# Weight tiles in a pool of their own at the bottom of SBUF, in a one-layer diffusion backbone with split fp32 matmuls

## The chip, the cores and the metric

The kernel runs on one core of one Trainium2 chip. The metric is the device time of one execution in microseconds (us), of which the median over several executions counts. A profile of one execution comes with it: every instruction with its start and duration, the clock that TensorE was granted, and the DMA traffic.

## The reference

One layer over 512 latent tokens of width 1024, with 256 context tokens beside them; everything is fp32.

```python
hx = modulate(rms_norm(x, norm1_g[i]), sh1, sc1)
qx, kx, vx, ux, gx = project(hx, w_in[i], q_norm_g[i], k_norm_g[i])
...
attn_x = block_attention(qx, concat([kc, kx]), concat([vc, vx]))
mix_x = merge_branches(attn_x, ux, gx, w_attn_out[i], conv_dw_w[i], ..., w_conv_out[i], w_out[i])
x = x + g1 * mix_x
hx2 = modulate(rms_norm(x, norm2_g[i]), sh2, sc2)
x = x + g2 * conv_glu_ffn(hx2, w_up[i], ffn_dw_w[i], ffn_dw_b[i], w_down[i])
return rms_norm(x, final_g)
```

`merge_branches` gates the attention branch and a convolution branch (GLU, width-31 depthwise convolution, layer norm, swish), and projects their sum. The feed forward goes up to two halves of 2816 channels, convolves one with width 3, and comes down again. The modulation (`sh1`, `sc1`, `g1`, `sh2`, `sc2`, `g2`) is a matrix-vector product.

## The kernel before

**Split operands.** TensorE multiplies in a 4-byte format with fewer significant bits than fp32. So each operand is split into two parts, `hi` and `lo`: ScalarE casts the source (L180), VectorE subtracts (L181). A product is then three matmuls, `mm3` (L203 to L205): hi by hi, hi by lo, lo by hi. A matmul has a stationary operand (`lhsT`, 128 columns, put into the array by a LDWEIGHTS of its own before each matmul) and a moving operand (`rhs`, mostly 512 columns). In the profile's names, `acc<-s,hl` is a matmul whose moving operand lies in a tile `s` and whose stationary operand lies in a tile `hl`.

**Where operands lie.** Activations live in 19 slots `s0` to `s18`, each [128, 2, 512] of 4 bytes, that is 4,096 bytes of each partition: 2,048 for hi, 2,048 for lo. Weights come as 1 MB chunks by DMA into `raw` (three buffers of 8,192 bytes, issued by SyncE) and are split into `hl` tiles, [128, 2, 1024], 8,192 bytes each, in four buffers taken in turn (`weights`, L191). Few more operands lie elsewhere: `ex`, `e0`, `e1` (three more slots for the gates and the feed forward), `y`, `plo`, `pT` (attention probabilities and parts of the values), `va`, `vb` (values).

**The order in the partition.** The allocator lays pools one behind the other in the order in which they are opened, and the tiles of a pool in the order in which they are first asked for. Pool `cst` is opened first and `wp` second. The build of the kernel before gives these byte offsets in each partition:

| what | pool | from | to | start modulo 64 |
|---|---|---|---|---|
| s0 to s18 | cst | 16,512 | 94,336 | 0 |
| cb0 to cb3 | cst | 94,336 | 111,232 | 0 |
| vecs, ident, ones, ..., va, vb, part | cst | 111,232 | 125,792 | va: 32 |
| raw, 3 buffers | wp | 125,792 | 150,368 | 32 |
| hl, 4 buffers | wp | 150,368 | 183,136 | 32 |
| y, 2 buffers | yp | 183,136 | 191,328 | 32 |
| ex, e0, e1 (among others) | rows, fp | 195,424 | 207,712 | 32 |

**The order of the work.** It is written out by hand. First the modulation, the normed rows `hx` (slots s0 to s7) and the first convolution channels; then k, v and q; then attention head by head, with the other half of q, the last convolution channels and the gates of branch a as fillers between the heads' steps, while VectorE runs the 124 taps of the convolution in what it has left; then the gates and branches; the output projection (`out_proj`, L903: stationary operand in `M`, the slots s0 to s7, moving operand in the slots s11 to s18, s8 to s10, in `ex` and in `hl`); then the feed forward in groups of 11, 7 and 4 channel tiles. In it, `up` (L968) has weights `hl` as the stationary and the slots s0 to s7 as the moving operand; `down` (L980) has channel slots `act` as the stationary operand (s8 to s18, then ex, e0, e1, then s8 again) and `hl` as the moving one. Dependencies between engines become semaphore waits that the framework writes; a buffer is handed on when its last reader is done.

Of the kernel before, what the change touches and what calls it, by code (L numbers as in the profile page):

```python
# [9 lines left out]
F32 = mybir.dt.float32  # L10
F32R = mybir.dt.float32r
# [4 lines left out]
P = 128  # L16
D = 1024
KT = D // P
T = 512
# [5 lines left out]
CT = CONV // P  # L25
TAPS = 31
# [6 lines left out]
GROUPS = ((0, 11), (11, 7), (18, 4))  # of the feed forward's channel tiles  # L33
CB = 2 * 512 + 32

# The order of the work: what keeps the tensor engine fed.
# start: m: modulation of two row tiles, x: tokens, r: rows, w: weights, a b: products
FIRST = "m0 x0 r0 m1 w0 a0 r1 m2 w1 r2 a1 b0 m3 r3 a2 b1 a3 b2 b3"
WHOLE = (("sh1", 0), ("sc1", 0), ("sc1", 1))  # modulation over the whole tensor engine
# q: query rows, u: a quarter of a channel tile | s: scores, f: filler  # L40
Q_ORDER = "quqqq|uusfufsfsfsf"
KV_LAG, Q_LAG = 3, 3  # of the transposes
# taps of the convolution: per step before attention, in a head's steps, in the gates'
# [3 lines left out]
EARLY, AHEAD = 48, 6  # the tap at which the second modulation starts, its loads before  # L47
HEAD_FILL = (2, 4, 5, 4, 5, 4, 4, 4)  # first step of a head with a filler
PV_FIRST = (3, 4, 5)  # heads with the values before the next scores
# gates' steps: the layer norm's stages, the second modulation's sums and results  # L50
# [4 lines left out]
# vecs columns  # L55
# [15 lines left out]
def layout(inp):  # L71
# [3 lines left out]
    # even members of a rotary pair first, within each head  # L75
# [69 lines left out]
    # rotary tables: constants of the shapes  # L145
# [14 lines left out]
def body(tc, x_d, ctx_d, wts_d, vecs_d, rows_d, rope_d, out_d, at):  # L160
# [9 lines left out]

    cst = pool("cst")
    wp = pool("wp")
    # [P, 2, T]: both parts of an operand of the tensor engine
    slot = [cst.tile([P, 2, T], F32R, name=f"s{i}") for i in range(19)]
    # convolution input and sum per channel tile; x before that, the residual after
    cbuf = [cst.tile([P, CB], F32, name=f"cb{i}") for i in range(CT)]

# [11 lines left out]
    done = []  # the latest weights' split  # L189

    def weights(name, w, n=CH):  # L191
        raw = fetch(name, n)
        out = []
        for o in range(0, n, 1024):
            m = min(1024, n - o)
            t = wp.tile([P, 2, 1024], F32R, tag="hl", name="hl", bufs=4)
            done[:] = split(raw[:, o : o + m], t[:, 0, :m], t[:, 1, :m])
            out.append(t[:, :, :m].rearrange("p a (k c) -> p a k c", c=w))
        return out
# [26 lines left out]
    def rsqrt(dst, ss, n, f=1.0):  # L226
        """dst = ((ss / n + eps) * f) ** -0.5"""
        V.tensor_scalar(dst, ss, f / n, f * EPS, ALU.mult, ALU.add)
        G.tensor_tensor(dst, dst, mhalf[:, : dst.shape[1]], ALU.pow)

    # silu of both conditioning vectors, side by side per row tile
# [5 lines left out]
    bs = cst.tile([P, 16], F32, name="bs")  # 1 + bias of the two scales  # L237
    V.tensor_scalar(bs[:, 0:8], vcol(V_BMOD + 8, 8), 1.0, None, ALU.add)
    V.tensor_scalar(bs[:, 8:16], vcol(V_BMOD + 32, 8), 1.0, None, ALU.add)
    cwh = vcol(V_CW, CT * TAPS)  # halved: the gate below is doubled  # L240
# [6 lines left out]
    def gemv_steps(part, r, k0, c):  # L247
        """part += sum over row tiles k0.. of r[:, k] * conditioning c"""
        for k in range(r.shape[1]):
            s = cs[:, k0 + k, c : c + 1]  # L250
            if k0 + k == 0:
                yield V.tensor_scalar(part, r[:, k], s, None, ALU.mult)
            else:
                yield V.scalar_tensor_tensor(part, r[:, k], s, part, ALU.mult, ALU.add)  # L254
# [12 lines left out]
    def half_row(name, jj):  # L267
        """Partial sums of 512 outputs of the modulation."""
        part = new_part()
        for h in range(2):  # L270
            raw = fetch((name, 2 * jj + h))
            gemv(part, raw.rearrange("p (k c) -> p k c", c=512), 4 * h, 0)
        return part
# [4 lines left out]
    def mod2(i):  # L278
        """Sixths of the modulation of the second half, with the first gate."""
        parts[i] = half_row(*sixths[i])  # L280
# [10 lines left out]
    def gate_row(pt, dst, part, j, f):  # L291
        """Half j of a gate, over all partitions; its bias is in dst."""
        PE.matmul(pt, lhsT=ones, rhs=part, start=True, stop=True)
        d = dst[:, 512 * j : 512 * j + 512]
        V.tensor_tensor(d, pt, d, ALU.add)
        if f != 1.0:
            V.tensor_scalar(d, d, f, None, ALU.mult)
# [7 lines left out]
    # ================= latent and context rows, q, k, v =================  # L305
# [6 lines left out]
    # values: both parts for the first group's heads  # L312
# [14 lines left out]
    mark = [None]  # the vector engine's latest step  # L327
# [4 lines left out]
    def head_scale(src, n, f, rs, junk):  # L332
        """rs: what scales each of n heads of src to unit rms (over sqrt(f))"""
        ss = small(4, "ssq")
        for h in range(n):
            S.activation(junk[:, tok(h)], src[:, tok(h)], AF.Square, accum_out=ss[:, h : h + 1])
        rsqrt(rs, ss[:, :n], HD, f)
# [9 lines left out]
    # queries stay as they are: their scale enters with the exponential  # L347
# [21 lines left out]
    with ExitStack() as p0:  # L369
# [4 lines left out]
        def kv_norm(src, s):  # L374
            """keys of token tile s (0-3 latent, 4-5 context), values alongside"""
            rs, qn = small(4, "rsq"), kt()
            head_scale(src, 2, 1.0, rs[:, :2], qn)
            for h in range(2):
                S.activation(qn[:, tok(h)], src[:, tok(h)], AF.Copy, scale=rs[:, h : h + 1])
            split(src[:, 256:384], vs[s][0], vlo[:, s])  # L380
            S.copy(vs[s][1], src[:, 384:512])
            if s < TT:
                return roped(qn, 2, s, TABk, kt(), qn)
            qn = heads(qn)
            mark[0] = V.tensor_tensor(qn, qn, gq[:, 1:2, :].broadcast_to([P, 2, HD]), ALU.mult).ins
            return qn
# [21 lines left out]
        # both conditioning vectors for a column tile of the tensor engine; the sum of the four  # L408
# [8 lines left out]
        def mod_rows(name, j):  # L417
            """256 outputs of the modulation, a row per conditioning vector; in each of the
            column tiles from two of the row tiles, or, while data is awaited, from all at once"""
            r = fetch((name, j)).rearrange("p (k c) -> p k c", c=256)  # L420
            pt = acc()
            if (name, j) in WHOLE:
                n = 2
                for k in range(KT):
                    PE.matmul(pt[0:n, 0:256], lhsT=cs[:, k], rhs=r[:, k], start=k == 0, stop=k == KT - 1)  # L425
            else:
                n = P
                for k in range(KT):
                    q = 32 * (k % 4)
                    PE.matmul(  # L430
                        pt[q : q + 32, 0:256], lhsT=cs4[:, k], rhs=r[:, k], start=k < 4, stop=k >= 4,
                        tile_position=(0, q),
                    )
            row = sp.tile([n, 256], F32, tag="row", name="row", bufs=2)
            V.tensor_copy(row, pt[0:n, 0:256])
            return row, sel if n == P else ident[0:2, 0:2]
# [6 lines left out]
        # the first channel tiles of the convolution branch follow the rows as they come  # L443
# [3 lines left out]
        def mod_x(j):  # L447
            """Modulation of channel tiles 2j and 2j+1."""
# [58 lines left out]
        # context rows  # L507
# [3 lines left out]
        # rotary tables with the gains  # L511
# [11 lines left out]
        def conv_taps():  # L523
            """depthwise over tokens, a tap at a time"""
# [8 lines left out]
        def conv_steps():  # L533
            """The taps, with the first sixth of the second modulation among them."""
# [15 lines left out]
        def conv(n):  # L550
            """The next n taps, queued behind the vector engine's latest step."""
            with tc.issue_after(mark[0]):
                for _ in range(n):
                    next(taps, None)
# [3 lines left out]
        # the first half of the weights in the places of q  # L558
# [15 lines left out]
        def tick():  # L574
            """The transposes that are due."""
# [60 lines left out]
    # ================= attention =================  # L636
    with ExitStack() as p1:
# [63 lines left out]
        def values(h, s, pT):  # L701
# [4 lines left out]
            if s == 5:  # L706
                split(pv[h], qT[h][:, 0], qT[h][:, 1])  # in the place of q
# [31 lines left out]
    # ================= gates, branches =================  # L739
# [38 lines left out]
    # layer norm over the convolution's channels, swish  # L778
# [20 lines left out]
    def ln_var(s_):  # L799
        """the variance as a column per token"""  # L800
# [7 lines left out]
    def ln_out(s_):  # L808
        """its power spread over the partitions again"""
# [74 lines left out]
    # ================= output projection (token major), residual =================  # L884
# [57 lines left out]
    # ================= feed forward =================  # L942
# [40 lines left out]
    def last_rows(t, w, f0, nf):  # L983
        """The last group's part, the final norm and the output."""
# [22 lines left out]
    # the first channel tiles start on the tokens that are ready  # L1007
# [52 lines left out]
```

## Time and profile before

| what | value |
|---|---|
| median of 3 runs | 852.66 us (852.2 to 852.67) |
| span of the profiled execution, first to last instruction | 851.1 us |
| median less this span | 1.6 us |
| matmuls, PE busy | 3948, 832.9 us (98% of the span) |
| VectorE busy | 566.6 us (67%) |
| ScalarE busy | 362.2 us (43%) |
| granted TensorE clock, mean over the span | 0.995 |

The profiled execution's own time is this span and what lies outside the first and the last instruction, 1.6 us if it was the median one. Matmuls are pipelined: one shows 395 ns from its start to its end, but the next starts about 230 ns after it. What a matmul costs TensorE is therefore the step from one start to the next. A row of the timeline gives starts to 0.01 us, so a step is read over many matmuls in a row.

### The profile page before, as it was taken

Reading aid. Unit: us, or ns where it says so; the run is one execution under the profiler, and the core shown is the slowest. Engines: PE = TensorE matmul, PEld = TensorE weight load, DVE = VectorE, ACT = ScalarE, POOL = GpSimd, SP = SyncE. Lnnn points to the kernel's source line nnn. Section 1 sums busy time; section 2 is a strip of 40 time slices with the busy share of each in tenths; the row PEclk is TensorE's granted clock in tenths of the full one; section 3 lists DMA queues with packets and bytes.
Section 4 is the critical chain, followed back from the end, with each engine's and each line's share of the span. In section 5 each row is a group of like instructions: output and inputs, shape, how many; then the busy total and the mean of one; then the engine's idle time right before and its main releaser. Section 6 shows DMA issues by size and latency. Waiting matters only on the chain.

```text
span 851.1 us, 10190 instructions
## 1 busy us (share of the span) xinstructions
PE 832.9 (98%) x3948; PEld 668.9 (79%) x3948; DVE 566.6 (67%) x979; ACT 362.2 (43%) x700; POOL 25.2 (3%) x50
## 2 busy tenths in 40 slices
PE   6999999999999999999999999999999999999996
PEld 3578888778888777888888988877888888888875
DVE  3478878999999996964854467745244555346555
ACT  4454455789776232423515643332122233213333
POOL 1001010000000000000000000000000000000001
PEclk9999999999999999999999999999999999999998
DMA  9861112020103345673730133432222222222102
GB/s 355 298 258 53 50 54 95 4 97 1 50 1 134 119 162 204 232 262 102 271 122 0 51 130 142 178 145 87 86 99 99 99 100 87 86 99 99 50 1 100
DMA packets 16177, 99.25 MB, mean 117 GB/s; under 512 B 1792, under 2 KB 2048, under 8 KB 6144
## 3 DMA queue, kind: packets, MB, share of 16 engines
q1 hardware_dynamic: 15120, 95.98, 30.7%
q10 hardware_dynamic: 1008, 2.62, 0.9%
q8 instruction: 31, 0.51, 0.2%
q14 instruction: 18, 0.15, 0.1%
HBM read 96.49 MB, written 2.10 MB: 116 GB/s over the span
## 4 chain that ended last, share of the span: by engine, by line
PE 92%; DVE 3%; ACT 2%; DMA 1%; issue 1%; POOL 0%; POOLq 0%; SPq 0%
PE acc L203 25%; PE acc L205 24%; PE acc L204 24%; PE bank L204 3%; PE bank L205 3%; PE bank L203 3%; PE tr L714 2%; DMA raw<-in_wts 1%; PE sc L203 1%; PE sc L205 1%; PE sc L204 1%; PE acc L425 1%; PE tr L402 1%; PE acc L430 1%; PE acc L265 0%
## 5 line engine op out<-in xcount | busy, mean ns | idle before, releaser
L203 PE MATMUL acc<-s,hl 128*128 128x512 f32 (+1 forms) x632 | 244.4, 388 | 0.6 <-ACT s L180 0.6
L204 PE MATMUL acc<-s,hl 128*128 128x512 f32 (+1 forms) x632 | 242.1, 383 | 0.0
L205 PE MATMUL acc<-s,hl 128*128 128x512 f32 (+1 forms) x632 | 242.0, 383 | 0.0
L181 DVE TENSOR_TENSOR hl<-raw,hl 128x1024 fp32r<-128x1024 f32 x118 | 139.0, 1184 | 79.1 <-ACT hl L180 78.9
L180 ACT CAST hl<-raw 128x1024 fp32r<-128x1024 f32 x118 | 119.7, 1022 | 153.6 <-PE acc L205 134.6
L203 PEld LDWEIGHTS acc<-s,hl 128*128 128x128 f32 x632 | 118.2, 188 | 27.1 <-ACT s L180 0.9
L204 PEld LDWEIGHTS acc<-s,hl 128*128 128x128 f32 x632 | 118.6, 188 | 26.2 <-issue 1.2
L205 PEld LDWEIGHTS acc<-s,hl 128*128 128x128 f32 x632 | 118.5, 188 | 25.9
L531 DVE SCALAR_TENSOR_TENSOR cb<-cb,vecs 128x512 f32<-128x512 f32 x120 | 88.3, 744 | 1.1
L203 PE MATMUL acc<-hl,s 128*128 128x512 f32 (+1 forms) x212 | 83.3, 393 | 0.2 <-DVE tmp L342 0.2
L204 PE MATMUL acc<-hl,s 128*128 128x512 f32 (+1 forms) x212 | 82.9, 391 | 0.0
L205 PE MATMUL acc<-hl,s 128*128 128x512 f32 (+1 forms) x212 | 82.8, 391 | 0.0
L960 DVE TENSOR_SCALAR tmp<-ap,vecs 128x512 f32<-128x512 f32 x22 | 12.0, 547 | 63.4 <-ACT ap L957 63.4
L957 ACT COPY ap<-acc 128x512 f32<-128x512 f32 x22 | 12.9, 588 | 81.0 <-PE acc L205 81.0
L205 PEld LDWEIGHTS acc<-hl,s 128*128 128x128 f32 x212 | 39.8, 188 | 9.3 <-DVE s L181 0.2
L203 PEld LDWEIGHTS acc<-hl,s 128*128 128x128 f32 x212 | 39.8, 188 | 9.2 <-PE sc L205 0.4
L204 PEld LDWEIGHTS acc<-hl,s 128*128 128x128 f32 x212 | 39.8, 188 | 8.9
L254 DVE SCALAR_TENSOR_TENSOR part<-raw,cs,part 128x512 f32<-128x512 f32 x56 | 41.9, 748 | 1.0
L181 DVE TENSOR_TENSOR s<-tmp,s 128x128 fp32r<-128x128 f32 (+2 forms) x67 | 29.1, 463 | 14.0 <-ACT s L180 13.8
L964 DVE TENSOR_TENSOR tmp<-tmp,acc 128x512 f32<-128x512 f32 x22 | 15.1, 685 | 30.7 <-PE acc L205 30.7
L651 ACT ACTIVATE pr<-sc,ss,qs 128x768 f32<-128x768 f32 x32 | 31.9, 998 | 5.5 <-DVE ss L650 3.6
L963 ACT ACTIVATE tmp<-tmp 128x512 f32<-128x512 f32 x22 | 13.9, 632 | 46.6 <-DVE tmp L962 46.6
(251 smaller groups left out, 1192.2 us busy)
## 6 DMA issues: line engine op xcount, KB each, us to landing
raw<-in_wts SPq DMA_DIRECT2D x78, 1024.0 KB, 4.8
raw<-in_wts SPq DMA_DIRECT2D x8, 768.0 KB, 4.2
cb<-in_x SPq DMA_DIRECT2D x8, 512.0 KB, 7.0
y<-in_ctx SPq DMA_DIRECT2D x2, 512.0 KB, 6.7
raw<-in_wts SPq DMA_DIRECT2D x2, 512.0 KB, 3.8
y<-in_rows ACTq DMA_DIRECT2D x2, 512.0 KB, 5.3
out<-o ACTq DMA_DIRECT2D x4, 256.0 KB, 2.8
out<-o SPq DMA_DIRECT2D x4, 256.0 KB, 2.6
```

The costliest lines, as they stand in the source:

```text
L180: a = S.copy(hi, src)
L181: b = V.tensor_tensor(lo, src, hi.bitcast(F32), ALU.subtract)
L203: PE.matmul(out, lhsT=l[0], rhs=r[0], start=start, stop=False)
L204: PE.matmul(out, lhsT=l[0], rhs=r[1], start=False, stop=False)
L205: PE.matmul(out, lhsT=l[1], rhs=r[0], start=False, stop=stop)
L254: yield V.scalar_tensor_tensor(part, r[:, k], s, part, ALU.mult, ALU.add)
L531: yield V.scalar_tensor_tensor(cacc[i], cin[i][:, j : j + T], w, cacc[i], ALU.mult, ALU.add)
L651: S.activation(pt, sc, AF.Exp, bias=mx, scale=r, accum_out=sm)
L714: PE.transpose(pt[:, tok(t)], pr[h, t][:, tok(s)], ident)
L957: S.copy(ap1[:, 1 : T + 1], a)
L963: S.activation(cv, cv, AF.Gelu_apprx_tanh)
L964: V.tensor_tensor(cv, cv, b, ALU.mult)
```

## The change

The `hl` tiles move from pool `wp` to a new pool `hlp`, which is opened before `cst`. Number of buffers, tags, shapes and instructions stay. The diff's other hunks drop comments and docstrings.

```diff
@@ body @@
+    hlp = pool("hlp")
     cst = pool("cst")
     wp = pool("wp")
-    # [P, 2, T]: both parts of an operand of the tensor engine
+
     slot = [cst.tile([P, 2, T], F32R, name=f"s{i}") for i in range(19)]
@@ weights @@
-            t = wp.tile([P, 2, 1024], F32R, tag="hl", name="hl", bufs=4)
+            t = hlp.tile([P, 2, 1024], F32R, tag="hl", name="hl", bufs=4)
```

By the allocator's order the offsets become, worked out by adding the 32,768 bytes of four hl tiles to what stood below them: hl 16,512 to 49,280; s0 to s18 49,280 to 127,104; the rest of `cst` and `raw` 32,768 further up, to 183,136. From there on (y, ex, e0, e1, pT and the rest) nothing moves. All of these shifts are multiples of 64 bytes, but for hl itself: it starts at 0 modulo 64, as the slots do.

## Rows read from the trace of the kernel before

**Rows 1.** The page: busy time by engine; the chain that ended last, by engine.
```profile
PE 832.9 (98%) x3948; PEld 668.9 (79%) x3948; DVE 566.6 (67%) x979; ACT 362.2 (43%) x700; POOL 25.2 (3%) x50
...
PE 92%; DVE 3%; ACT 2%; DMA 1%; issue 1%; POOL 0%; POOLq 0%; SPq 0%
```

**Rows 2.** Groups by line and shape, TensorE: moving,stationary, count, busy, mean duration.
```profile
L203 PE MATMUL acc<-s,hl 128*128 128x512 f32 x568 | 227.2, 400 | 0.0
...
L203 PE MATMUL acc<-hl,s 128*128 128x512 f32 x204 | 81.1, 397 | 0.2 <-DVE tmp L342 0.2
...
L203 PE MATMUL bank<-hl,s 128*128 128x512 f32 x48 | 19.3, 402 | 0.0
...
L203 PE MATMUL acc<-s,hl 128*128 128x256 f32 x64 | 17.3, 282 | 0.6 <-ACT s L180 0.6
...
L203 PE MATMUL bank<-s,hl 128*128 128x512 f32 x32 | 13.0, 406 | 0.0
...
L203 PE MATMUL acc<-hl,e 128*128 128x512 f32 x16 | 6.3, 391 | 0.0
...
L203 PE MATMUL acc<-hl,s 128*128 128x256 f32 x8 | 2.2, 280 | 0.0
```

**Rows 3.** Timeline of TensorE, feed forward, down: start, duration, one matmul a row.
```profile
606.11 0.40 PE L203 MATMUL acc<-hl,s 128*128 128x512 f32 x1
...
608.91 0.40 PE L203 MATMUL acc<-hl,s 128*128 128x512 f32 x1
```

**Rows 4.** Timeline of TensorE, output projection, one row tile and one half.
```profile
439.29 0.40 PE L203 MATMUL acc<-s,s 128*128 128x512 f32 x1
...
441.33 0.40 PE L203 MATMUL acc<-ex,s 128*128 128x512 f32 x1
...
444.13 0.40 PE L203 MATMUL acc<-hl,s 128*128 128x512 f32 x1
```

**Rows 5.** Timeline of TensorE, feed forward's second group, down.
```profile
740.01 0.39 PE L204 MATMUL acc<-hl,e 128*128 128x512 f32 x1
...
740.92 0.40 PE L205 MATMUL acc<-hl,e 128*128 128x512 f32 x1
```

**Rows 6.** Timeline of TensorE, start of the output projection.
```profile
422.43 0.39 PE L203 MATMUL acc<-s,s 128*128 128x512 f32 x1
...
424.97 0.39 PE L205 MATMUL acc<-s,s 128*128 128x512 f32 x1
...
427.24 0.39 PE L203 MATMUL acc<-s,s 128*128 128x512 f32 x1
```

**Rows 7.** Busy time by engine in a stretch of slot by slot.
```profile
458.40:465.00 6.60, 6.60 (x31) 5.47 (x30) 3.38 (x11) 4.50 (x15) 0.55 (x1) 1.00 0.00 0
```

**Rows 8.** TensorE instructions that touch hl, by stage: length, busy (count), clock, DMA.
```profile
0.00:49.00 49.00, 14.91 (x52) 0.97 0.88 335
49.00:155.00 106.00, 79.91 (x331) 1.00 0.21 79
155.00:291.00 136.00, 56.30 (x220) 1.00 0.16 59
291.00:422.00 131.00, 125.78 (x530) 1.00 0.55 201
422.00:471.00 49.00, 14.04 (x64) 1.00 0.18 65
471.00:596.00 125.00, 122.89 (x612) 1.00 0.34 125
596.00:652.00 56.00, 56.00 (x241) 1.00 0.25 89
652.00:736.00 84.00, 84.00 (x362) 1.00 0.26 94
736.00:842.50 106.50, 106.50 (x470) 1.00 0.19 70
```

**Rows 9.** Busy time by engine in the attention stage: PE, PEld, DVE, ACT, POOL.
```profile
155.00:291.00 136.00, 134.88 (x715) 111.31 (x714) 131.25 (x249) 98.83 (x186) 2.02 (x2) 1.00 0.16 59
```

**Rows 10.** Timeline of VectorE and of TensorE around the layer norm's two sums.
```profile
310.52 0.69 DVE L783 TENSOR_TENSOR ln<-ln,cb 128x512 f32<-128x512 f32 x1
...
321.74 0.68 DVE L783 TENSOR_TENSOR ln<-ln,cb 128x512 f32<-128x512 f32 x1
...
314.64 1.02 PE L792 MATMUL acc<-ln,ones 128*128 128x512 f32 x2
326.70 0.95 PE L265 MATMUL acc<-ones,ln 128*128 128x1 f32 x8
```

## The prediction

> **What bounds the kernel now.** I read the page first: its busy times and the chain that ended last. TensorE is busy 98% of the span and holds 92% of the chain; no other engine holds more than 3% of it [rows 1]. So the time is made of the steps from one matmul to the next, and a change of place can matter in two ways: through that step, or through the few places where TensorE waits. I then read the groups by shape, to see which operands meet [rows 2]: most matmuls have one operand in a slot and the other in an hl tile. A group's mean is a duration and not a step, so it doesn't answer; the timeline does.
>
> In the feed forward's down, 12 steps take 608.91 − 606.11 = 2.80 us, 233.3 ns each, with hl moving and a slot stationary [rows 3]. In the output projection, 9 steps of slot by slot take 441.33 − 439.29 = 2.04 us, 226.7 ns each. The 12 that follow in the same accumulation, with ex or hl moving against a slot, take 444.13 − 441.33 = 2.80 us, again 233.3 ns [rows 4]. Nothing but the tiles changes between those two runs. The reverse is there too: in the feed forward, where down's stationary operand is for once e0 or e1 and the moving one hl, four steps take 740.92 − 740.01 = 0.91 us, 227.5 ns [rows 5].
>
> What sets these pairs apart can be read from the offsets in the layout. Slot by slot: both start at 0 modulo 64 bytes, and both lie below 94,336. hl by e: both start at 32 modulo 64, and both lie above 150,368. hl or ex by slot: one at 32 and high, the other at 0 and low. Pairs alike take 226.7 ns, unlike pairs 233.3 ns. The trace of before can't tell alignment from region, since here the two go together. The change gives hl both of the slots' properties, so for the forecast it needn't.
>
> **The price.** 233.3 − 226.7 = 6.7 ns for each matmul of 512 columns with hl on one side and a slot on the other. Their number: (568 + 204 + 48 + 32) times the three lines of mm3 = 2,556 [rows 2]. Ceiling: 2,556 × 6.67 ns = 17.0 us. The 64 × 3 matmuls of 256 columns in that view, and 24 more with hl moving at the end, have no alike run to compare; by columns half of it, 3.3 ns, some 0.7 us; nothing is the lower bound. Against it stand the 48 matmuls of hl by e [rows 2], which become unlike: up to 48 × 6.67 = 0.3 us lost.
>
> Not every one of them gets the whole. A run of alike pairs needs some matmuls to settle: at the start of the output projection 11 steps take 424.97 − 422.43 = 2.54 us, 231 ns each, and the 10 behind them 2.27 us, 227 ns [rows 6]. A settled step saves 6.7 ns, one while settling 2.4 ns. So I go by stage, with the counts of instructions that touch hl [rows 8] at 6.67 ns (a 256-column one at half), and take off what short runs cost:
>
> - Feed forward, 471 to 842.5: 612 + 241 + 362 + 470 = 1,685, of which 216 are of 256 columns: 9.8 + 0.7 = 10.5 us at most. Runs are of hundreds of matmuls, broken in the second group's down by ex, e0 and e1, by the two gate products and by 256 columns. I take 8.7 us for 512 columns and 0.4 for 256.
> - Start, 0 to 155: 383, at most 2.6 us. Long runs in u, k and q, but with transposes between: 1.8.
> - Attention, 155 to 291: 220, at most 1.5 us. They come in pieces of 12 between transposes and scores, so nearly all are settling: 220 × 2.4 ns = 0.5.
> - Gates and branches, 291 to 422: 530, at most 3.5 us; some follow ex or ones products, or stand before the stage's long runs: 2.5.
> - Output projection: 64, at most 0.4; broken by ex in each run: 0.2.
>
> Sum: 9.1 + 1.8 + 0.5 + 2.5 + 0.2 = 14.1 us.
>
> **What the shorter steps run into.** TensorE gets ahead of engines whose work stays the same. In the attention stage VectorE is busy 131.25 of 136 us [rows 9], so it has 4.8 us left, more than the 0.5 asked for, but little of it at each step. Past 291 the layer norm is next: its first sum ends on VectorE at 311.2 and TensorE takes it at 314.6, 3.4 us of slack; the second ends at 322.4 and is taken at 326.7, 4.3 us [rows 10]. The 0.5 of attention and the part of 2.5 that is earned before don't use that up. Elsewhere the split of hl has a lead of buffers: ScalarE and VectorE work one buffer in four, and in the feed forward they have room. I take off 1.2 us for waits of this kind, mainly in the start and in attention, where 2.3 us of the sum lie; nothing and 2.3 are its bounds. Left: 12.9 us.
>
> Other edits cost nothing. No instruction, wait or buffer is added: four buffers before, four after, released by the same readers. Slots, constants, cb and raw move by 32,768 bytes, a multiple of 64, so pairs among them stay alike or unlike as they were; the cast and the subtraction that write hl stand on engines that TensorE doesn't wait for from 422 on; before that a change in them would be paid by VectorE in the attention stage. The dropped comments do nothing.
>
> The Trainium skill has a rule against all of this. On the page "TensorE: Matmul & The Clock Gate", section "Step-by-step: what each phase is for", it says that the moving operand and the weight load have independent read ports, so that loading the next weights doesn't take bandwidth from the running matmul; and its section "Back-to-back issue gap" gives N / 2.4 + 2.5 ns, 215.8 ns for 512 columns wherever they lie. By it the sum would be 0. The trace disagrees: 226.7 and 233.3 ns, by tiles [rows 3, 4].
>
> **The sum.** The profiled execution's span is 851.1 us; with the 1.6 us outside it that is the median, 852.66. 852.66 − 12.9 = 839.8; I say 840.
>
> **Rivals.**
>
> *Region decides, and its border lies under the slots' new top.* Slots below 94,336 are known to be quick with each other; now they reach to 127,104. If the border lies just above 94,336, s11 to s18 fall on the other side and hl on the lower. Up keeps its gain (slots s0 to s7; 22 × 48 matmuls, 864 of them of 512 columns: 5.8 us, and 0.4), and so does what meets s0 to s10 elsewhere; down with s11 to s18, branch a and part of k and v keep 233.3, and the 96 matmuls of the output projection whose moving operand is s11 to s18 lose 0.6 us. That leaves about 8.5 us: 844. For it: nothing in the trace excludes it. Against: the offsets fit alignment as well.
>
> *The gain before the feed forward is taken by VectorE and the DMA queue.* VectorE is at 97% in attention [rows 9], and the first 49 us are loads at 0.88 of the DMA engines [rows 8]. If all stages up to 422 give nothing, 9.1 + 0.2 are left, less 0.3: 9 us, 843.7. Against: the slack in [rows 10].
>
> *The place does nothing.* If the step belongs to something that slot by slot has in common besides its place, hl keeps 233.3 and the time stays 852.7. Against it: the two runs within one accumulation [rows 4], and hl by e [rows 5], which is quick amid slow ones. The Trainium skill's rule above would give this rival.
>
> *Slower.* Today hl is written high while most reads of TensorE's other operand go low. Afterwards ScalarE's and VectorE's writes into hl fall into the region from which TensorE reads both operands. If a write stretched an alike step beyond an unlike one, the change would lose: at 236 ns a step it costs 2,556 × 2.7 ns = 6.9 us, 859.6; it decides from 233.3 ns on. Against it: in a stretch of slot by slot ScalarE was busy 4.50 and VectorE 3.38 of 6.60 us, splitting into slots, and 31 matmuls were in flight [rows 7]: 29 steps of 227 ns and the two that reach in from its ends.
>
> **Chances.** Forecast 0.62 (its own range 835 to 842, the lower end by the ceiling 17.8 us); region with a border 0.15; gain before the feed forward lost 0.08; nothing 0.11; slower 0.04. The likeliest gives 840. The range reaches down to the ceiling, 835, and up past both partial cases, to 848, where the two would meet or the border's cost is double what I worked out; unchanged and slower are left out, 0.15, and some 0.03 beyond. Within 0.2%, 1.7 us, is what a measurement here can't tell from no change: faster 0.85, same 0.11, slower 0.04.
>
> **What would show it.** In the new profile: 226.7 ns steps in down and up over tens of matmuls; unlike steps left where ex, e0 or e1 meets hl or a slot; about 9 us less from 471 to the last matmul, 2 to 3 less between 291 and 422, little in attention. Region with a border: down at 233 with s11 to s18 and at 227 with s8 to s10. Wrong altogether: 233 ns everywhere in up. If up is quick and the time isn't lower by 9 us or more, TensorE waits somewhere that it didn't.

## The result, and the profile after

The changed kernel takes 839.32 us (median of 4 runs, 838.52 to 840.19), the kernel before 852.62 (4 runs, 852.2 to 852.67). The ratio is 0.9838, 95% interval 0.9821 to 0.9855: 13.3 us less, where 12.9 were forecast.

The page of the changed kernel, span and busy time by engine:

```profile
span 836.7 us, 10190 instructions
...
PE 818.0 (98%) x3948; PEld 669.3 (80%) x3948; DVE 566.5 (68%) x979; ACT 362.1 (43%) x700; POOL 25.2 (3%) x50
```

Beside [rows 1], nothing changes but TensorE: the same 3948 matmuls, 14.9 us less busy, and it is still busy 98% of the span. VectorE and ScalarE have the same work to 0.1 us. So the time came out of the matmuls' steps and no engine took TensorE's place.

The timeline of TensorE, feed forward, down, hl moving and a slot stationary (the diff moved the lines of the kernel by one):

```profile
598.03 0.39 PE L205 MATMUL acc<-hl,s 128*128 128x512 f32 x1
...
600.98 0.39 PE L206 MATMUL acc<-hl,s 128*128 128x512 f32 x1
```

13 steps in 2.95 us, 226.9 ns each, where [rows 3] have 233.3. In the output projection, the stretch of [rows 4]:

```profile
433.05 0.39 PE L204 MATMUL acc<-s,s 128*128 128x512 f32 x1
...
435.08 0.40 PE L204 MATMUL acc<-ex,s 128*128 128x512 f32 x1
...
435.79 0.39 PE L204 MATMUL acc<-hl,s 128*128 128x512 f32 x1
...
437.83 0.39 PE L204 MATMUL acc<-hl,s 128*128 128x512 f32 x1
```

Slot by slot is as it was, 9 steps in 2.03 us; the three with ex moving are still slow, 0.71 us together, about 235 ns each; the nine with hl moving behind them take 2.04 us, 226.7 ns, and were at 233.3. And hl by e of [rows 5], which was alike and is no longer, has become slow: six steps take 1.40 us, 233.3 ns each:

```profile
727.10 0.40 PE L204 MATMUL acc<-hl,e 128*128 128x512 f32 x1
...
728.50 0.39 PE L204 MATMUL acc<-hl,s 128*128 128x512 f32 x1
```

By stage, the view of [rows 8] for the changed kernel, cut at the same instructions (length, busy and count of what touches hl, granted clock, DMA):

```profile
0.00:48.05 48.05, 14.98 (x53) 1.00 0.88 341
48.05:152.26 104.21, 78.16 (x330) 1.00 0.22 81
152.26:287.57 135.31, 55.52 (x219) 1.00 0.16 59
287.57:415.69 128.12, 122.91 (x530) 1.00 0.56 205
415.69:464.59 48.90, 13.82 (x64) 1.00 0.17 65
464.59:587.38 122.79, 120.68 (x613) 1.00 0.35 127
587.38:641.78 54.40, 54.40 (x242) 1.00 0.26 92
641.78:723.38 81.60, 81.60 (x362) 1.00 0.28 97
723.38:827.80 104.42, 104.42 (x470) 1.00 0.20 71
```

Subtracting the lengths, with the four stages of the feed forward as one, gives:

| stage (before) | before | after | gain | forecast, before waits |
|---|---|---|---|---|
| 0 to 155 | 155.0 | 152.3 | 2.7 | 1.8 |
| attention | 136.0 | 135.3 | 0.7 | 0.5 |
| gates and branches | 131.0 | 128.1 | 2.9 | 2.5 |
| output projection | 49.0 | 48.9 | 0.1 | 0.2 |
| feed forward to the last matmul | 371.5 | 363.2 | 8.3 | 9.1 |
| behind it | 8.6 | 8.9 | −0.3 | 0 |

These sum to 14.4 us, the difference of the two profiled spans; the medians lie 13.3 apart. About 1 us of the 14.4 is in the first 48 us, where only 53 matmuls touch hl, and it goes with TensorE's clock and not with the change. In the execution of before the granted clock fell there for a while, and in that of the changed kernel it didn't. The stretch from 15 to 25 us, before, after, in run 1 and in run 9 below (busy time of PE, PEld, DVE, ACT, POOL, then granted clock, DMA share and GB/s):

```profile
15.00:25.00 10.00, 8.62 (x52) 4.70 (x51) 3.78 (x13) 4.40 (x6) 1.13 (x6) 0.83 0.82 327
15.00:25.00 10.00, 8.29 (x57) 4.42 (x56) 4.58 (x16) 4.46 (x6) 1.38 (x6) 1.00 0.82 324
15.00:25.00 10.00, 8.62 (x53) 4.96 (x53) 4.23 (x15) 4.47 (x7) 1.38 (x6) 0.83 0.85 325
15.00:25.00 10.00, 8.60 (x58) 4.41 (x56) 4.59 (x15) 4.46 (x6) 1.38 (x6) 1.00 0.84 327
```

A clock of 0.83 over 10 us is 3.4 us at the lower of its two levels, 1.2 GHz, and the rest at 2.4 (0.17 × 10 / 0.5). The fall comes with either step: run 1 has the quick steps of the changed kernel and the fall, run 9 has slow steps and no fall. The matmul that starts at 49.09 us before starts at 48.03 in the changed kernel, at 49.48 in run 1 and at 48.34 in run 9. Without this share the spans differ by some 13.4 us, as the medians do.

### The profile page after: what moved, and what is told of

Its sections match the earlier page's. It is cut to its first block, busy times and chain, and to the rows that moved or that the text cites. A ratio compares the mean times of both kernels' runs of the same rounds, so it can differ in the third digit from the quotient of the medians.

```text
span 836.7 us, 10190 instructions
## 1 busy us (share of the span) xinstructions
PE 818.0 (98%) x3948; PEld 669.3 (80%) x3948; DVE 566.5 (68%) x979; ACT 362.1 (43%) x700; POOL 25.2 (3%) x50
## 4 chain that ended last, share of the span: by engine, by line
PE 91%; DVE 4%; ACT 2%; DMA 1%; issue 1%; POOL 0%; POOLq 0%; SPq 0%
PE acc L204 24%; PE acc L206 24%; PE acc L205 24%; PE bank L205 3%; PE bank L206 3%; PE bank L204 3%; PE tr L715 2%; DMA raw<-in_wts 1%; PE sc L204 1%; PE sc L206 1%; PE sc L205 1%; PE acc L426 1%; DVE s L182 1%; PE acc L431 1%; PE tr L403 1%
## 5 line engine op out<-in xcount | busy, mean ns | idle before, releaser
L204 PE MATMUL acc<-s,hl 128*128 128x512 f32 (+1 forms) x632 | 242.0, 384 | 0.6 <-ACT s L181 0.6
L206 PE MATMUL acc<-s,hl 128*128 128x512 f32 (+1 forms) x632 | 239.5, 379 | 0.0
L205 PE MATMUL acc<-s,hl 128*128 128x512 f32 (+1 forms) x632 | 239.3, 379 | 0.0
L204 PE MATMUL acc<-hl,s 128*128 128x512 f32 (+1 forms) x212 | 82.3, 388 | 0.2 <-DVE tmp L343 0.2
L206 PE MATMUL acc<-hl,s 128*128 128x512 f32 (+1 forms) x212 | 81.9, 387 | 0.0
L205 PE MATMUL acc<-hl,s 128*128 128x512 f32 (+1 forms) x212 | 81.9, 386 | 0.0
L958 ACT COPY ap<-acc 128x512 f32<-128x512 f32 x22 | 12.9, 588 | 77.9 <-PE acc L206 77.9
L182 DVE TENSOR_TENSOR s<-tmp,s 128x128 fp32r<-128x128 f32 (+2 forms) x67 | 29.2, 465 | 14.5 <-ACT s L181 14.4
```

Source lines behind the costliest of these rows:

```text
L182: b = V.tensor_tensor(lo, src, hi.bitcast(F32), ALU.subtract)
L204: PE.matmul(out, lhsT=l[0], rhs=r[0], start=start, stop=False)
L205: PE.matmul(out, lhsT=l[0], rhs=r[1], start=False, stop=False)
L206: PE.matmul(out, lhsT=l[1], rhs=r[0], start=False, stop=stop)
L958: S.copy(ap1[:, 1 : T + 1], a)
```

## Experiments

The trace of before left two readings: alignment, or region of the partition. All runs below compute the full layer; only offsets in SBUF differ. Each was timed beside the kernel before on the same chip; a ratio is the run's time over that kernel's, with its 95% interval in brackets. A pad is a small tile that is written once and moves all that lies behind it (the L-numbers shift with its lines).

**1. hl high, but aligned.** The kernel before, with

```diff
+            if not done:
+                G.memset(wp.tile([P, 8], F32, name="pad0"), 0.0)
             t = wp.tile([P, 2, 1024], F32R, tag="hl", name="hl", bufs=4)
...
+    pad1 = pool("pad1")
+    G.memset(pad1.tile([P, 8], F32, name="pad1"), 0.0)
     yp = pool("yp")
```

> The kernel before with 32 empty bytes ahead of the four hl tiles and 32 behind them: hl stays high in the partition (150,400 on) but starts at 0 modulo 64 like the slots. If alignment decides: settled steps of hl against a slot at 226.7 ns, time 838 to 841, as the changed kernel. If the region decides: steps at 233.3 ns, time 852 to 853.

The time is 840.39 us against 853.03, ratio 0.9863 (0.9834 to 0.9893). Down, hl by slot, the stretch of [rows 3]:

```profile
597.23 0.39 PE L207 MATMUL acc<-hl,s 128*128 128x512 f32 x1
...
601.08 0.39 PE L206 MATMUL acc<-hl,s 128*128 128x512 f32 x1
```

17 steps in 3.85 us, 226.5 ns. Nothing moved into another region, and the gain is there.

**2. hl low, but misaligned.** The changed kernel, with

```diff
+    pad0 = pool("pad0")
+    G.memset(pad0.tile([P, 8], F32, name="pad0"), 0.0)
     hlp = pool("hlp")
+    pad1 = pool("pad1")
+    G.memset(pad1.tile([P, 8], F32, name="pad1"), 0.0)
```

> The changed kernel with 32 empty bytes ahead of the hl tiles and 32 behind them: hl lies low (16,544 on) but starts at 32 modulo 64, while the slots keep 0. If alignment decides: 233.3 ns a step, time 852 to 853. If the region decides: 226.7 ns, time 838 to 841.

The time is 853.02 us against 853.03, ratio 1.0003 (0.9993 to 1.0013). The same place in down, 44 steps in 10.26 us, 233.2 ns:

```profile
601.62 0.40 PE L210 MATMUL acc<-hl,s 128*128 128x512 f32 x1
...
611.88 0.40 PE L209 MATMUL acc<-hl,s 128*128 128x512 f32 x1
```

The low place alone is worth nothing, nor is the move of everything else by 32 KiB. With run 1 this settles it: alignment, and not region. What has to be aligned to what is left to the runs below.

**3. One pad.** The kernel before, with

```diff
     G.memset(mhalf, -0.5)
+    G.memset(cst.tile([P, 8], F32, name="pad0"), 0.0)
```

> The kernel before with 32 empty bytes among the small constants, behind mhalf: hl stays high, and everything behind the pad, hl, ex, e0, e1, y, pT, va, raw, comes to 0 modulo 64. If alignment decides: 226.7 ns for hl by slot and for ex, e0, e1 by slot or by hl too, so 0.3 to 1 us less than the changed kernel: 838 to 840. If the region decides: 852 to 853.

The time is 839.59 us, ratio 0.984 (0.9826 to 0.9855). Now ex, e0 and e1 are quick with hl as well; from a step with s8 across ex, e0 and e1 to s8 again, 12 steps take 2.72 us, 226.7 ns:

```profile
726.66 0.39 PE L203 MATMUL acc<-hl,s 128*128 128x512 f32 x1
...
729.38 0.39 PE L203 MATMUL acc<-hl,s 128*128 128x512 f32 x1
```

So 32 bytes in the old place give what the move gave. The further 0.3 to 1 us that ex, e0 and e1 were to bring can't be seen beside the changed kernel's 839.32.

**4. Slots off instead of hl on.** The kernel before, with

```diff
+    G.memset(cst.tile([P, 8], F32, name="pad0"), 0.0)
     slot = [cst.tile([P, 2, T], F32R, name=f"s{i}") for i in range(19)]
     cbuf = [cst.tile([P, CB], F32, name=f"cb{i}") for i in range(CT)]
+    G.memset(cst.tile([P, 8], F32, name="pad1"), 0.0)
```

> The kernel before with 32 empty bytes ahead of the slots and 32 behind cb: slots at 32 modulo 64, hl where it was, also at 32. If only the offset of the two operands to each other counts: 226.7 ns, 838 to 841. If each operand has to start at a multiple of 64 by itself: 233.3 ns or more, also slot by slot, 852 to 854. If the region decides: 852 to 853 with slot by slot still at 226.7.

The time is 838.98 us, ratio 0.9835 (0.982 to 0.985). Both operands start at 32 modulo 64, and down runs 18 steps in 4.08 us, 226.7 ns:

```profile
596.75 0.39 PE L205 MATMUL acc<-hl,s 128*128 128x512 f32 x1
...
600.83 0.39 PE L205 MATMUL acc<-hl,s 128*128 128x512 f32 x1
```

So neither operand needs an alignment of its own. What counts is the distance between the two.

**5. A distance of 64.** The changed kernel with the pads of run 2 at `[P, 16]`: hl 64 bytes below a slot, modulo 256.

> The changed kernel with 64 empty bytes ahead of the hl tiles and 64 behind them: hl at 64 modulo 128, slots at 0 modulo 128. If the period is 64 bytes: 226.7 ns a step, 838 to 841. If it is 128 or more: 233.3 ns, 852 to 853.

The time is 846.7 us, ratio 0.9939 (0.9921 to 0.9956): between the two, and neither expectation held. In up (slot moving, hl stationary), 44 steps take 10.08 us, 229.1 ns each. The nine steps of down (hl moving) just before it take 2.10 us, 233.3 ns each:

```profile
651.67 0.40 PE L208 MATMUL acc<-hl,s 128*128 128x512 f32 x1
...
653.77 0.39 PE L208 MATMUL acc<-s,hl 128*128 128x512 f32 x1
...
663.85 0.39 PE L210 MATMUL acc<-s,hl 128*128 128x512 f32 x1
```

The period is more than 64 bytes, and the two forms differ.

**6 and 7. Four distances at once.** The changed kernel with hl tiles of 8,224 bytes, so that the four buffers stand at four offsets; run 6 uses them from byte 16 on, run 7 from their start:

```diff
-            t = hlp.tile([P, 2, 1024], F32R, tag="hl", name="hl", bufs=4)
+            t = hlp.tile([P, 2056], F32R, tag="hl", name="hl", bufs=4)[:, 4:2052]
+            t = t.rearrange("p (a c) -> p a c", a=2)
```

> The changed kernel with hl tiles of 8,224 bytes, used from their byte 16 on: the four buffers start at 16, 48, 16, 48 modulo 64, 16 bytes to one side or the other of a multiple of 32. If only a multiple of 64 counts as alike: 233.3 ns or more, 852 or more. If whole 16-byte lines are enough: 226.7 ns, 838 to 841. If the cost grows with the distance from 64: about 230 ns, 845 to 847.

> The changed kernel with hl tiles of 8,224 bytes, used from their start: buffers at 0, 32, 0, 32 modulo 64, so that every other weight tile is alike to the slots. By alignment, half of the gain of 13.3 us, less some settling at each change of tile: 846 to 848. If one unlike operand spoiled whole stretches: 850 to 853.

Run 6 takes 848.49 us, ratio 0.9956 (0.9941 to 0.9971), which lies in none of its three ranges. Run 7 takes 851.98 us, ratio 0.9989 (0.9979 to 0.9999). Its first expectation took for granted that 0 and 64 are the same, and fails. The time is in the range of the second, but the rows below don't show whole stretches spoiled: the step changes from tile to tile. No buffer of run 7 stands at a multiple of 256 bytes from the slots; they stand at 32, 64, 96 and 128.

In up each hl tile serves 24 matmuls in a row, so the last rows of successive tiles give one step length for each distance. Run 7, four tiles:

```profile
523.75 0.40 PE L207 MATMUL acc<-s,hl 128*128 128x512 f32 x1
...
529.36 0.39 PE L207 MATMUL acc<-s,hl 128*128 128x512 f32 x1
...
534.95 0.39 PE L207 MATMUL acc<-s,hl 128*128 128x512 f32 x1
...
540.55 0.39 PE L207 MATMUL acc<-s,hl 128*128 128x512 f32 x1
...
546.04 0.40 PE L207 MATMUL acc<-s,hl 128*128 128x512 f32 x1
```

Run 6, four tiles:

```profile
525.82 0.39 PE L207 MATMUL acc<-s,hl 128*128 128x512 f32 x1
...
531.42 0.40 PE L207 MATMUL acc<-s,hl 128*128 128x512 f32 x1
...
536.87 0.39 PE L207 MATMUL acc<-s,hl 128*128 128x512 f32 x1
...
542.43 0.39 PE L207 MATMUL acc<-s,hl 128*128 128x512 f32 x1
...
547.96 0.39 PE L207 MATMUL acc<-s,hl 128*128 128x512 f32 x1
```

The differences over 24 belong, in this order, to the distances 96, 128, 32 and 64 in run 7 and 112, 16, 48 and 80 in run 6. A distance here is the start of the moving slot less the start of the hl tile, modulo 256, by the builds' offsets:

| distance | 16 | 32 | 48 | 64 | 80 | 96 | 112 | 128 |
|---|---|---|---|---|---|---|---|---|
| ns a step | 227.1 | 233.3 | 231.7 | 228.8 | 230.4 | 233.8 | 233.3 | 232.9 |

The table holds for up, where the slot moves. In run 6's down hl moves, so its distances are −16, −48, −80 and −112, and none of them is quick: 240 steps take 55.93 us, 233.0 ns each:

```profile
594.30 0.39 PE L205 MATMUL acc<-hl,s 128*128 128x512 f32 x1
...
650.23 0.40 PE L205 MATMUL acc<-hl,s 128*128 128x512 f32 x1
```

**8. Low, and all alike.** The changed kernel with the pad of run 3.

> The changed kernel with 32 empty bytes behind mhalf, so that ex, e0, e1, y, pT and va come to 0 modulo 64 too. By alignment 0.3 to 1 us less than the changed kernel, 838 to 839.5, which a run can hardly tell; hl by e and ex by hl at 226.7 ns in its trace. If the region adds something to alignment, less than the high, all alike kernel's 839.6 by more than 1 us.

The time is 838.96 us, ratio 0.9844 (0.983 to 0.9859). It is as quick as runs 3 and 4 and the changed kernel, and its trace has hl by e at 226.7 ns, as expected; a difference of half a microsecond can't be told, so the region adds nothing that can be seen. No version beat the changed kernel by more than a measurement can tell.

**9. A distance of 128 throughout.** The changed kernel, with

```diff
     hlp = pool("hlp")
+    pad1 = pool("pad1")
+    G.memset(pad1.tile([P, 32], F32, name="pad1"), 0.0)
```

> The changed kernel with 128 empty bytes between hl and the slots: the distance of hl to a slot is 128 modulo 256 everywhere. If the period is 256 bytes (or 512): about 233 ns a step, as the buffer at 128 showed in the run with every other buffer, 851 to 853. If it is 128 and that buffer was disturbed by its neighbours: 226.7 ns, 838 to 841.

The time is 851.95 us, ratio 0.9973 (0.9957 to 0.9989). In up 32 steps take 7.43 us, 232.2 ns each, and the 20 of down before them 4.65 us, 232.5 ns:

```profile
651.79 0.40 PE L207 MATMUL acc<-hl,s 128*128 128x512 f32 x1
...
656.44 0.39 PE L206 MATMUL acc<-s,hl 128*128 128x512 f32 x1
...
663.87 0.39 PE L208 MATMUL acc<-s,hl 128*128 128x512 f32 x1
```

So 128 isn't a period. Runs 1 and 3 had hl at 256 modulo 512 from the slots and were quick, the changed kernel at 0: 256 is enough.

**10. The other sign.** The kernel before, with the first pad of run 1 at `[P, 24]` and no second one: hl 64 bytes above a slot.

> The kernel before with 96 empty bytes between raw and hl: hl stands 64 bytes above a slot, modulo 256, where the run off by 64 had it 64 below. If the sign of moving less stationary decides: the two forms swap, hl moving by slot at about 229 and slot moving by hl at 233.5 ns, 849 to 851. If only the distance decides: the same steps as in that run, 846 to 848. If 64 is only half unlike for both: 230 ns in both forms, 845 to 847.

The time is 850.82 us, ratio 0.9959 (0.9941 to 0.9978), where the sign theory expected it. With the slot moving the step is slow, as it foresaw: from 499.74 on, 50 steps in 11.67 us, 233.4 ns. With hl moving, at a distance of 64 now, the step is not one value: 42 steps in 9.80 us, 233.3 ns, in the first group's down, and 42 in 9.61, 228.8, in the last group's:

```profile
499.74 0.39 PE L205 MATMUL acc<-s,hl 128*128 128x512 f32 x1
...
511.41 0.39 PE L207 MATMUL acc<-s,hl 128*128 128x512 f32 x1
...
605.75 0.40 PE L205 MATMUL acc<-hl,s 128*128 128x512 f32 x1
...
615.55 0.40 PE L205 MATMUL acc<-hl,s 128*128 128x512 f32 x1
...
822.65 0.39 PE L205 MATMUL acc<-hl,s 128*128 128x512 f32 x1
...
832.26 0.39 PE L205 MATMUL acc<-hl,s 128*128 128x512 f32 x1
```

With the slot moving the sign counts: up runs at 233.4 ns here, at −64, and at 229.1 in run 5, at 64. With hl moving it isn't decided, since at 64 a stretch can settle at either of two steps.

## Why the prediction was right, step by step

- *Alike pairs 226.7, unlike 233.3 ns, and the change makes hl by slot alike.* Right, and in both directions: hl by slot came down, hl by e went up. The rows that carried it were the two runs inside one accumulation [rows 4].
- *Alignment or region, left open.* Runs 1 and 2 decide for alignment, so the rival of a border under the slots' new top falls. The changed kernel's trace says so too: 240 steps of the first group's down, which goes through s8 to s18, take the 54.40 us from 587.38 on, 226.7 ns each.
- *0 or 32 modulo 64.* This reading of the property was too coarse. Run 4 shows that it is the distance of the two operands, runs 5, 7 and 9 that 64 and 128 bytes are no period; whole multiples of 256 bytes are quick in every run that has them. The change moved hl to a multiple of 512 from the slots, so the forecast didn't suffer. Since the reasoning asked for a multiple of 64 only, that was luck. For a place 64 bytes further on, the same reasoning would have promised the whole gain, and run 5 got 6.3 of some 13 us.
- *The sum.* It was 14.1 us before waits, against some 13.4 in the spans without the clock's share and 13.3 in the medians. The feed forward was put at 9.1 and gave 8.3. The term of the 256-column matmuls had the wrong sign. Before, 54 of them take 6.30 us, 116.7 ns; after, 56 take 6.72, 120.0 ns:

```profile
470.77 0.28 PE L205 MATMUL acc<-s,hl 128*128 128x256 f32 x1
...
477.07 0.28 PE L205 MATMUL acc<-s,hl 128*128 128x256 f32 x1
```

```profile
463.75 0.28 PE L204 MATMUL acc<-s,hl 128*128 128x256 f32 x1
...
470.47 0.28 PE L206 MATMUL acc<-s,hl 128*128 128x256 f32 x1
```

  With 216 of them that is up to 216 × 3.3 ns = 0.7 us lost, where 0.4 was to be gained and nothing was called the lower bound. The 512-column steps of the stage thus gave up to 8.3 + 0.7 = 9.0 us, with the loss of hl by e in it, against 8.7.
- *1.2 us for waits.* Not seen. TensorE's time without a matmul, span less busy time, is 18.2 us before and 18.7 after. In each stage up to 422 the gain is what was summed for it or more, in the first also without the clock's share, and in attention too, where VectorE is as busy as before, 130.92 of 135.31 us. That the total came out so near the medians is partly luck: the 1.2 us taken off for waits made up for the 256 columns, which were off by up to 1.1 us the other way.
- *The place does nothing*, which the Trainium skill's rule on independent read ports ("TensorE: Matmul & The Clock Gate", "Step-by-step: what each phase is for") would give: falls. Run 2 is the changed kernel with two pads of 32 bytes, and takes 13.7 us more. As far as the step goes, the trace disagrees with the rule. The Trainium skill's formula that the prediction cites beside it (same page, "Back-to-back issue gap") is given there for a single matmul by itself, so its 215.8 ns is no figure for this stream, and no stretch above is as quick.
- *Slower*: the writes into hl's new region cost nothing that a run shows; run 2, with hl in the same region, takes as long as the kernel before.

What stays open: which of the two reads gives way, that of the moving operand or that of the weights for the next matmul, and why a stretch at a distance of 64 settles at 228.8 or at 233.3 ns. No run here separates the reads. All of it was measured with one 4-byte format and a weight load before each matmul; no run shows how other formats behave.

## What to carry to other kernels

Where TensorE is the bound, read the step from start to start over tens of matmuls, by pairs of tiles, and compare it with the quickest pair of the same shape in the kernel: a difference of 3% that follows the tiles and not the stage can be a matter of offsets, and a pad of a few bytes tests it. In a kernel like this one, give both operands of large matmuls starts that differ by multiples of 256 bytes. One pad of 32 bytes was worth 13 us here, as much as moving the pool, since hl stood 32 bytes short of such a multiple. Price each shape from its own rows, since the 256-column ones went the other way.

## What the runs showed of the hardware that was not expected

- The step of a 512-column matmul depends on the distance between its operands' start offsets in the partition. It is 226.7 ns at a multiple of 256 bytes. With the slot moving it is 227.1 at 16, 228.8 at 64, 233.3 at 32 and about 232.5 at 128 (runs 6, 7 and 9). The distance has a sign: with the slot moving, −64 gave 233.4 (run 10). Neither the region nor the alignment of one operand by itself matters (runs 1, 2 and 4).
- For 256 columns the order of two distances is the reverse: 120.0 ns at a multiple of 256, 116.7 at 32 (changed kernel and kernel before).
- The same distance can settle at two steps: 64 bytes with hl moving gave 233.3 and 228.8 ns in one execution (run 10).
- TensorE's granted clock can fall early in the program in one execution and not in another, with quick steps (run 1 against the changed kernel) as with slow ones (the kernel before against run 9). From 15 to 25 us it was 0.83 or 1.00, which is about 1 us in the profiled span.
